# Regrouped start, adaLN rows, gates and boundary work in a two-layer hybrid transformer kernel, with the latent mean of each norm issued inside the last-but-one product

## The chip, the cores and the metric

The kernel runs on one core of one Trainium2 chip. The metric is the device time of one execution in microseconds. Before the change, three timed runs gave a median of 2119.14 us (2117.68 to 2120.08).

The core has five engines that run their own instruction streams: TensorE (PE in the profile, with PEld for its weight loads), VectorE (DVE), ScalarE (ACT), GpSimd (POOL) and SyncE (SP). An instruction waits in its engine's stream until the semaphores it names are reached, and everything behind it on that engine waits too. SP issues the transfers of almost all weights, POOL the transfers of the adaLN matrix.

## The reference

Two layers work on 256 latent tokens and 256 context tokens of width 1024. Cut to what matters:

```python
sc, scc = jax.nn.silu(c), jax.nn.silu(c_ctx)
for l in range(DEPTH):                                   # DEPTH = 2
    mod = (sc @ w_ada[l] + b_ada[l]).reshape(B, 1, 9, D) # and mod_c from scc, for the context
    h  = ffn_half_step(h, g_ffn1[l], mod[:,:,0], mod[:,:,1], mod[:,:,2], ...)   # and hc
    u  = modulate(rmsnorm(h, g_mix[l]), mod[:,:,3], mod[:,:,4])                 # and uc
    y, yc = token_mixer(u, uc, ...)      # u @ w_in -> attention, pooling, gated linear attention (GLA),
                                         # 3 x 1024 sigmoid gates; branches gated, summed, @ w_out
    h  = h + mod[:,:,5] * y                                                     # and hc, not in the last layer
    h  = ffn_half_step(h, g_ffn2[l], mod[:,:,6], mod[:,:,7], mod[:,:,8], ...)   # and hc, not in the last layer

def ffn_half_step(h, g, shift, scale, gate, w1, w3, w2):  # FF = 2816
    u = modulate(rmsnorm(h, g), shift, scale)
    return h + 0.5 * gate * ((silu(u @ w1) * (u @ w3)) @ w2)
```

Everything is float32. The output is the latent stream h.

## The kernel before, in words

**Layout.** The residual stream `h` lies transposed in SBUF: 8 tiles of 128 channels (k = 0..7), each with 512 columns, latent tokens first, context tokens behind. A product with a weight runs in three passes (`mm3`, lines 235 to 240): every float32 operand is split into a high part (made by ACT, line 190) and the rest (made by DVE, line 202), and TensorE adds high by high (L238), low of the data by high of the weight (L239), high of the data by low of the weight (L240). Data tiles are called uhi/ulo, hi/lo or oph/opl, weight tiles whi/wlo.

**Weights.** The class `Weights` is a planner: it records the order in which units of weights are asked for, and then loads ahead (SP issues the transfer into one of four raw buffers) and cuts ahead (ACT makes whi, DVE makes wlo) as long as the number of cut tiles stays under `room`. The rooms are `ROOM_FFN`, `ROOM_MIX`, and for the first FFN `ROOM_1` and `ROOM_2`. A framework with a list scheduler orders the instructions of each engine; it follows the order of the program text except where a dependency or a lower priority says otherwise. So a statement's place in the text decides where its instructions stand in each engine's queue.

**Stages.** In each layer ffn1, mixer, ffn2. An FFN runs 22 blocks of up-projections (`up`) in two halves, each followed by 8 down-products (`down`) that add to h (`grow`). The last two down-products, k = 6 and 7, run over the latent columns first and over the context columns second.

**Norms.** `grow` squares the new h tile on ACT and adds it to `acc` on DVE (L492). When h is complete, one product with a constant matrix gives the mean, `ms` (L508), ACT makes `rstd` from it (Ln, Exp), DVE makes `ut` (L517), ACT `uhi`, DVE `ulo` (L521). `norm_ahead` does the mean and rstd of the latent half while the context half of the last two products still runs; it is called after product k = 6 of the context span. The mixer's `out_last` does the same.

**adaLN.** `mod` needs 36 blocks (l, j) of 512 columns of `w_ada`. A generator (`ada_all`) does them in order, and calls of `adas(n)` all over the program move it n steps. The first four (l = 0, j < 4) are done on TensorE from rows loaded by SP: 8 float32 products 32x512 per block (L370), an ACT copy `adaev`, four transposes `ada2` (L384) and a DVE reduction. All the others are done on DVE (`adaacc`, L403, two per 128 rows) from rows loaded by POOL, with one 128x32 product at the end (L424), except those in the table `EDGE`: blocks (0,17) and (1,17) are done on TensorE like the first four, spread over the first products of ffn2 of each layer.

**Mixer.** Three generators are driven side by side: attention, GLA and a filler that spends TensorE's spare time on products of `w_in` and of the branches (psum tiles `fill`, `pool`). A table of credits `FILL` says how many filler steps go between two steps of attention or GLA; `GATES` says how many of the 8 middle gates (and 4 output gates) may be filled in before the pooling result is there. While the filler waits for attention (`len(self.oa) < 4`), it has nothing to give.

**The last FFN** covers the latent tokens only. Between its blocks 0 to 3 and the rest it transposes h to token-major (16 transposes, L715, copied by ACT into `ht`) and spreads the gate over the tokens (`gt`, L728).

## Time and profile before

| what | value |
|---|---|
| timed runs | 2119.14 us median (2117.68 to 2120.08) |
| profiled execution | 2120.19 us, span 2118.4 us |
| TensorE busy | 2071.1 us, 98% of the span |
| VectorE busy | 1449.1 us, 68% |
| ScalarE busy | 883.3 us, 42% |
| GpSimd busy | 138.4 us, 7% |
| granted TensorE clock, mean | 0.994 |

Times in the trace are counted from the start of the span. A group row reads: line, engine, operation, result from operands, shapes, count, busy time, mean duration in ns, idle time of the engine ahead of it and what ended it. Products are pipelined, so one that is shown 0.39 us long may start 0.23 us after the one before; a float32 (not split) product has two records.

### The profile page before, as it was taken

The page shows a single profiled execution, that of the slowest core. Times are in us where ns is not written, and L with a number is a line of the kernel's source. Part 1 is how long each engine was busy: PE and PEld are TensorE (multiplying, and loading weights), DVE is VectorE, ACT ScalarE, POOL GpSimd, SP SyncE. Part 2 cuts the span into 40 slices and gives each one's busy share as a digit, 9 for nine tenths or more (in the row PEclk, how much of TensorE's full clock was granted, in tenths as well). Part 3 has the DMA queues.
Part 4 walks back from the last instruction along what each step waited for, and adds up shares of the span by engine and source line. Part 5 has one row for each costly group of instructions (what it writes and reads, how often), then busy time and mean ns, then how long its engine had stood idle before and what let it go on. Part 6 is the DMA issues. An engine that isn't in the chain of part 4 may idle for free.

```text
span 2118.4 us, 30235 instructions
## 1 busy us (share of the span) xinstructions
PE 2071.1 (98%) x11308; PEld 1738.7 (82%) x11308; DVE 1449.1 (68%) x2876; ACT 883.3 (42%) x1805; POOL 138.4 (7%) x264
## 2 busy tenths in 40 slices
PE   7999999999999999999999999999999999998999
PEld 4888888977777888788888898888888887897997
DVE  4789588875877664766965886685554688665564
ACT  5423223464445553432322343322343566654452
POOL 0011011000100000101110100010000000000000
PEclk9999999999999999999999999999999999999999
DMA  9557456424423223445744645473451343565663
GB/s 319 150 157 206 125 170 169 118 59 122 137 75 83 67 70 95 130 139 139 216 132 131 173 125 154 110 224 114 121 151 36 102 119 85 140 169 145 182 205 121
DMA packets 416836, 290.48 MB, mean 137 GB/s; under 512 B 18608, under 2 KB 388912, under 8 KB 416688
## 3 DMA queue, kind: packets, MB, share of 16 engines
q1 hardware_dynamic: 395920, 221.22, 37.0%
q0 software_dynamic: 20480, 67.13, 11.1%
q8 instruction: 89, 1.46, 0.3%
q14 instruction: 59, 0.48, 0.1%
q10 hardware_dynamic: 288, 0.20, 0.0%
HBM read 287.44 MB, written 1.05 MB: 136 GB/s over the span
## 4 chain that ended last, share of the span: by engine, by line
PE 52%; issue 41%; DMA 3%; DVE 2%; POOL 1%; ACT 0%; SPq 0%; POOLq 0%; DVEq 0%; ACTq 0%
PE ps L238 14%; PE ps L240 14%; PE ps L239 14%; DMA raw<-in_w_ada_dram 2%; PE fill L238 2%; PE fill L240 2%; PE fill L239 2%; DMA ada<-in_w_ada_dram 1%; POOL raw L355 1%; PE sc L1145 1%; DVE adaacc L403 1%; PE ada L370 1%; PE pt L1163 0%; PE av L1181 0%; DVE wlo L202 0%
## 5 line engine op out<-in xcount | busy, mean ns | idle before, releaser
L202 DVE TENSOR_TENSOR wlo<-raw,whi 128x512 fp32r<-128x512 f32 (+4 forms) x912 | 532.5, 618 | 103.3 <-ACT whi L190 92.0
L238 PE MATMUL ps<-uhi,whi 128*128 128x512 f32 (+1 forms) x1584 | 555.4, 353 | 7.8 <-ACT uhi L190 7.8
L239 PE MATMUL ps<-ulo,whi 128*128 128x512 f32 (+1 forms) x1584 | 554.8, 351 | 0.2 <-DVE ulo L560 0.2
L240 PE MATMUL ps<-uhi,wlo 128*128 128x512 f32 (+1 forms) x1584 | 554.5, 351 | 0.0
L190 ACT ACTIVATE whi<-raw 128x512 fp32r<-128x512 f32 (+4 forms) x912 | 467.7, 567 | 173.6 <-DMA raw<-in_ffn_w_dram 53.7
L238 PEld LDWEIGHTS ps<-uhi,whi 128*128 128x128 f32 x1584 | 299.6, 190 | 54.1 <-ACT uhi L190 12.0
L240 PEld LDWEIGHTS ps<-uhi,wlo 128*128 128x128 f32 x1584 | 300.7, 190 | 46.1 <-issue 5.8
L239 PEld LDWEIGHTS ps<-ulo,whi 128*128 128x128 f32 x1584 | 300.9, 190 | 40.6 <-issue 1.9
L403 DVE SCALAR_TENSOR_TENSOR adaacc<-raw,csil,adaacc 128x512 f32<-128x512 f32 x420 | 303.9, 746 | 32.7 <-DMA raw<-in_w_ada_dram 32.1
L238 PE MATMUL ps<-hi,whi 128*128 128x512 f32 (+1 forms) x738 | 271.2, 368 | 1.5 <-ACT hi L190 1.5
L240 PE MATMUL ps<-hi,wlo 128*128 128x512 f32 (+1 forms) x738 | 269.9, 366 | 0.0
L239 PE MATMUL ps<-lo,whi 128*128 128x512 f32 (+1 forms) x738 | 269.6, 366 | 0.0
L190 ACT ACTIVATE silu<-ps 128x512 f32<-128x512 f32 (+1 forms) x88 | 47.8, 543 | 495.7 <-PE ps L240 495.7
L355 POOL DMA_DIRECT2D raw<-in_w_ada_dram x256 | 137.4, 537 | 1783.2 <-DVE adaacc L401 713.7
L659 DVE TENSOR_TENSOR silu<-silu,ps 128x512 f32<-128x512 f32 (+1 forms) x88 | 54.5, 619 | 245.7 <-PE ps L240 140.0
L238 PE MATMUL fill<-uhi,whi 128*128 128x512 f32 (+1 forms) x576 | 204.2, 355 | 3.9 <-ACT whi L190 3.9
L240 PE MATMUL fill<-uhi,wlo 128*128 128x512 f32 (+1 forms) x576 | 196.7, 342 | 0.2 <-DVE wlo L202 0.2
L239 PE MATMUL fill<-ulo,whi 128*128 128x512 f32 (+1 forms) x576 | 196.2, 341 | 0.0
L238 PEld LDWEIGHTS ps<-hi,whi 128*128 128x128 f32 x738 | 139.1, 189 | 24.0 <-ACT hi L190 1.7
L239 PEld LDWEIGHTS ps<-lo,whi 128*128 128x128 f32 x738 | 139.2, 189 | 22.6 <-DVE lo L202 0.2
L240 PEld LDWEIGHTS ps<-hi,wlo 128*128 128x128 f32 x738 | 139.2, 189 | 22.6
L238 PEld LDWEIGHTS fill<-uhi,whi 128*128 128x128 f32 x576 | 110.0, 191 | 26.2 <-issue 8.5
(279 smaller groups left out, 2304.8 us busy)
## 6 DMA issues: line engine op xcount, KB each, us to landing
raw<-in_ffn_w_dram SPq DMA_DIRECT2D x192, 512.0 KB, 4.7
raw<-in_w_ada_dram POOLq DMA_DIRECT2D x256, 256.0 KB, 3.4
raw<-in_w_in_dram SPq DMA_DIRECT2D x86, 512.0 KB, 4.5
raw<-in_ffn_w_dram SPq DMA_DIRECT2D x48, 384.0 KB, 4.4
raw<-in_ffn_w_dram SPq DMA_DIRECT2D x48, 320.0 KB, 3.8
raw<-in_w_branch_dram SPq DMA_DIRECT2D x48, 256.0 KB, 2.9
ada<-in_w_ada_dram SPq DMA_DIRECT2D x32, 256.0 KB, 5.4
raw<-in_w_out_dram SPq DMA_DIRECT2D x16, 512.0 KB, 5.0
```

The costliest lines, as they stand in the source:

```text
L190: i = self.nc.scalar.activation(**k)
L202: second = lambda: self.nc.vector.tensor_tensor(out=lo, in0=src, in1=f32hi, op=ALU.subtract)
L238: mm(out, wh, xh, start=start, stop=False)
L239: mm(out, wh, xl, start=False, stop=False)
L240: mm(out, wl, xh, start=False, stop=stop)
L355: self.nc.gpsimd.dma_start(out=t, in_=src)
L370: nc.tensor.matmul(ps[32 * g:32 * g + 32, :], self.csil[:, k, :], self.early[j][k] if early else unit.hi, start=(k < 4), stop=(k >= 4))
L403: nc.vector.scalar_tensor_tensor(out=acc[s], in0=unit.hi, scalar=c, in1=acc[s], op0=ALU.mult, op1=ALU.add)
L659: nc.vector.tensor_tensor(out=s[:, 0:n], in0=s[:, 0:n], in1=p3[:, 0:n], op=ALU.mult)
L1145: nc.tensor.matmul(sc[:, 0:nk], q[h][:, tt * P:(tt + 1) * P], keys[h][:, k0:T], start=True, stop=True)
```

## The change

The change does seven things.

1. **Start.** SiLU of the conditioning vector is made from Exp and DVE operations and not from the Silu table. The first adaLN block, the transposes that set up h, and the transposes of the normalised input come in another order, and the early adaLN blocks are tied into that order by dependencies. `ROOM_1` is 12, and the third unit of weights of the second half is asked for after k = 2 of the first products (`more`).
2. **Rows.** `EDGE` is empty: blocks (0,17) and (1,17) go through the DVE generator like the others.
3. **Gates.** `GATES` of mixer 0 is (4, ...) where it was 2. In mixer 1 a new `LATER` lets gates 0 to 7 and 16 to 23 run while the filler waits for attention.
4. **Boundary.** In the last FFN, the 16 transposes of h (`by_tokens`) come ahead of the norm, and the gate's products come after block 7 and not after block 3.
5. **Latent mean.** `norm_ahead` is called at f = 5 of 11 within the context span of down-product k = 6, and at k = 5 of 8 in the mixer's last output products, not after that product.
6. `ROOM_MIX` becomes a pair with the same two values.
7. Line numbers move: 190 becomes 191, 202 becomes 203, 238 to 240 become 239 to 241, 370 becomes 384, 384 becomes 400, 403 becomes 417, 508 becomes 522.

Three places in the engines' streams. First ScalarE at the start of the program, around the last two of the four early adaLN blocks (adaev; uhi is the first FFN's data, raw to whi the cutting of its weights). Before:

```order
L190 ACTIVATE whi<-raw 128x512 x2
L190 ACTIVATE uhi<-hr,mod_170,am_1_172 128x256 x6
L190 ACTIVATE whi<-raw 128x512 x4
L190 ACTIVATE adaev<-ada 128x512 x2
L190 ACTIVATE uhi<-hr,mod_170,am_1_172 128x256 x8
L190 ACTIVATE whi<-raw 128x512 x10
```

and after the change:

```order
L191 ACTIVATE whi<-raw 128x512 x2
L191 ACTIVATE uhi<-hr,mod_170,am_1_172 128x256 x6
L191 ACTIVATE whi<-raw 128x512 x2
L191 ACTIVATE adaev<-ada 128x512
L191 ACTIVATE whi<-raw 128x512 x6
L191 ACTIVATE adaev<-ada 128x512
L191 ACTIVATE uhi<-hr,mod_170,am_1_172 128x256 x8
L187 ACT_TABLE_LOAD
```

The first of the two adaev copies moved ahead of two cuts, the second moved behind four more. The six whi between them cut the three units of weights that follow.

Second TensorE in mixer 0, where the queries' norms (qsum) are turned (rq). Before:

```order
L238 MATMUL q<-hi,whi 128x512
L239 MATMUL q<-lo,whi 128x512
L240 MATMUL q<-hi,wlo 128x512
L1102 MATMUL qsum<-sqq,cst 32x512 x4
L1131 MATMUL rq<-cst_72,rq 128x128 x4
L238 MATMUL pool<-hi,whi 128x512
```

and after the change (the rows between these two pieces are further fill products, 24 in all between qsum and rq):

```order
L240 MATMUL q<-lo,whi 128x512
L241 MATMUL q<-hi,wlo 128x512
L1128 MATMUL qsum<-sqq,cst 32x512 x4
L239 MATMUL fill<-uhi,whi 128x512
L240 MATMUL fill<-ulo,whi 128x512
```

```order
L240 MATMUL fill<-ulo,whi 128x512
L241 MATMUL fill<-uhi,wlo 128x512
L1157 MATMUL rq<-cst_72,rq 128x128 x4
L239 MATMUL pool<-hi,whi 128x512
L240 MATMUL pool<-lo,whi 128x512
```

Two whole gates now stand between the sums and the turn.

Third TensorE at the boundary from mixer 1 to the last FFN, from the last output product (hilo) to the first up-products (uhi). Before:

```order
L240 MATMUL ps<-hilo,wlo 128x256
L508 MATMUL ms<-acc,cst_72 128x256
L370 MATMUL ada<-raw,csil 32x512 x3
L238 MATMUL ps<-uhi,whi 128x256 x4
L239 MATMUL ps<-ulo,whi 128x256
```

and after the change:

```order
L241 MATMUL ps<-hilo,wlo 128x256
L770 MATMUL ps<-cst_72,h 128x128 x16
L522 MATMUL ms<-acc,cst_72 128x256
L239 MATMUL ps<-uhi,whi 128x256 x3
L240 MATMUL ps<-ulo,whi 128x256
```

The adaLN products are gone from here (five more of them further on too), and the transposes of h stand where they were not before. At the same boundary of layer 0, the eight products of block (0,17) are gone in the same way.

The diff, cut to its core:

```diff
-ROOM_1, ROOM_2, LAST = 16, 36, 4
+ROOM_1, ROOM_2, LAST = 12, 36, 4
-GATES = (2, 12)
-EDGE = {(1, 17): (1, 2), (0, 17): (0, 2)}
+GATES = (4, 12)
+LATER = (0, 16)
+EDGE = {}
...
-        self.act(out=self.csil[:, :, 0:2], in_=self.vec[0][:, V_C:V_C + 16].rearrange("p (s k) -> p k s", s=2), func=AF.Silu)
+        c, e = self.vec[0][:, V_C:V_C + 16], self.tiny(16, "esil")
+        self.act(out=e, in_=c, func=AF.Exp, scale=-1.0)
+        nc.vector.tensor_scalar(out=e, in0=e, scalar1=1.0, scalar2=None, op0=ALU.add)
+        nc.vector.reciprocal(out=e, in_=e)
+        by_k = lambda t: t.rearrange("p (s k) -> p k s", s=2)
+        nc.vector.tensor_tensor(out=self.csil[:, :, 0:2], in0=by_k(c), in1=by_k(e), op=ALU.mult)
...
-        self.residual(range(4), [normed])
+        self.residual(range(6), (normed, last))
+        self.adas(4)
...
+        self.residual(range(6, KD))
+        self.xin = None
+        self.adas(1)
...
             self.evac = self.act(out=ev, in_=ps, func=AF.Copy)
-            if not early or j in (1, 3):
-                yield
+            yield
...
             self.w.room = ROOM_1
             first[0].extend(part(0, [2]))
-            first[1].extend(part(1, [0]))
+
+            def more():
+                self.adas(1)
+                self.w.room = 2 * ROOM_1
+                first[1].extend(part(1, [0, 1, 2]))
 
             def rest():
                 self.adas(1)
                 next(norm)
                 self.w.room = ROOM_2
-                first[1].extend(part(1, [1, 2]))
+                self.w.run_ahead()
 
         else:
             self.w.room = ROOM_FFN
+            ht = self.by_tokens() if final else None
...
-                    if c.start and k == 6:
-                        self.norm_ahead(l, i)
+                        if c.start and k == 6 and f == 5:
+                            self.norm_ahead(l, i)
...
-        up(0, 4)
+        up(0, 8)
+
         assert {(l, 8, 0), (l, 8, 1)} <= self.have
-
-        ht = []
-        ...
-        up(4, KF)
+        up(8, KF)
...
-                    if c.start and dc == dcs[0]:
-                        self.norm_ahead(l, 3)
+                        if c.start and dc == dcs[0] and k == 5:
+                            self.norm_ahead(l, 3)
...
+        later = [gate(j) for j in (*range(8), *range(16, 24))][0:LATER[l]]
         while len(self.oa) < 4:
-            yield 1
+            if later:
+                yield from later.pop(0)
+            else:
+                yield 1
...
-        for dc in range(4):
-            yield from gate(16 + dc)
+        for dc in range(4 if self.full else 8):
+            if 16 + dc not in self.gates:
+                yield from gate(16 + dc)
```

More of the change, by code (lines that the diff above doesn't have):

```diff
@@ L149, in __init__ @@
         self.have = set()
-        self.ahead = self.seconds = None
+        self.ahead = self.seconds = self.products = None
         self.after, self.owed, self.on_pe, self.edge = iter(()), 0, False, []
@@ L239, in mm3 @@
         mm(out, wh, xl, start=False, stop=False)
-        mm(out, wl, xh, start=False, stop=stop)
+        self.last_product = mm(out, wl, xh, start=False, stop=stop)
     def parts(self, src, n=T):
@@ L304, in setup @@
             self.act(out=f, in_=f, func=AF.Ln, scale=1.0 / D, bias=self.eps[:, 0:1])
-            self.act(out=f, in_=f, func=AF.Exp, scale=-0.5)
+            last = self.act(out=f, in_=f, func=AF.Exp, scale=-0.5)
             xr.append([self.slot(name="xr") for _ in range(2)])
@@ L367, in ada @@
                 for k in range(2 * u, 2 * u + 2):
+                    g = k % 4
                     unit = None if early else self.ada_unit(l, j, k)
-                    g = k % 4
-                    nc.tensor.matmul(ps[32 * g:32 * g + 32, :], self.csil[:, k, :], self.early[j][k] if early else unit.hi,
-                                     start=(k < 4), stop=(k >= 4))
+                    others = [self.last_product] if j in (1, 3) and not k else [self.products] if k else []
+                    self.products = nc.tensor.matmul(ps[32 * g:32 * g + 32, :], self.csil[:, k, :], self.early[j][k] if early else unit.hi,
+                                                     start=(k < 4), stop=(k >= 4))
+                    if early and self.tc:
+                        self.behind(self.products, others)
                     if unit:
@@ L621, in ffn @@
             self.adas(5)
-            self.residual(range(4, KD))
-            self.xin = None
-            self.adas(5)
             part = lambda half, ms: [self.both((w1, w3), 4 * half, m * P) for m in ms]
@@ L665, in up @@
                     if begin:
-                        steps = [lambda: None, lambda: self.adas(4), lambda: self.adas(1), lambda: self.adas(4), rest]
+                        steps = [lambda: None, lambda: self.adas(4), more, lambda: self.adas(4), rest]
                         o = self.dense_first(first, u, steps)
@@ L706, in ffn @@
             return
-        up(0, 4)
+        up(0, 8)
         assert {(l, 8, 0), (l, 8, 1)} <= self.have
-        ht = []
-        for j in range(2):
-            for c in range(2):
-                ps = self.ps()
-                for k in range(4):
-                    nc.tensor.transpose(ps[:, k * P:(k + 1) * P], self.h[:, 4 * c + k, j * P:(j + 1) * P], self.ident)
-                t = self.slot(name="ht")
-                self.act(out=t, in_=ps, func=AF.Copy)
-                ht.append(t)
         gt = []
@@ L753, in ffn, with by_tokens @@
         self.w.done(*us)
+    def by_tokens(self):
+        nc = self.nc
+        ht = []
+        for j in range(2):
+            for c in range(2):
+                ps = self.ps()
+                for k in range(4):
+                    nc.tensor.transpose(ps[:, k * P:(k + 1) * P], self.h[:, 4 * c + k, j * P:(j + 1) * P], self.ident)
+                t = self.slot(name="ht")
+                self.act(out=t, in_=ps, func=AF.Copy)
+                ht.append(t)
+        return ht
     def mixer(self, l):
@@ L761, in mixer @@
         self.l, self.full, self.n = l, full, n
[L762 removed]
+        self.w.room = ROOM_MIX[l]
         def load(t):
```

30 lines of the change are left out of this document (15 added, 15 removed).

## The prediction

> **What bounds the kernel now.** I read the page's busy times and its chain first, then TensorE's waits, then the granted clock in short windows.
>
> ```profile
> PE 2071.1 (98%) x11308; PEld 1738.7 (82%) x11308; DVE 1449.1 (68%) x2876; ACT 883.3 (42%) x1805; POOL 138.4 (7%) x264
> PE 52%; issue 41%; DMA 3%; DVE 2%; POOL 1%; ACT 0%; SPq 0%; POOLq 0%; DVEq 0%; ACTq 0%
> ```
>
> TensorE is busy for 98% of the span, and the chain lies on TensorE or on its issuing for 93%. So time comes off in three ways only: fewer instructions on TensorE, fewer waits of TensorE, or less time at a lowered clock. The waits (engine, line, what it waited for: total us, times, longest):
>
> ```profile
> PE ps L238 <- ACT uhi L190: 7.8, 6, 1.8
> PE ada L370 <- DMA raw<-in_w_ada_dram: 4.1, 2, 3.2
> PE fill L238 <- ACT whi L190: 3.9, 1, 3.9
> PE ms L508 <- DVE acc L492: 3.7, 1, 3.7
> PE rq L1131 <- ACT rq L190: 3.2, 1, 3.2
> PE ot L1383 <- DVE mx L1149: 1.7, 1, 1.7
> PE o L1367 <- DVE st L1352: 1.2, 1, 1.2
> ```
>
> These are small sums, but four of them are single waits over 3 us, and each of these costs more than itself. The windows show it (us, busy time of each engine, granted clock, DMA share, GB/s):
>
> ```profile
> 495.00:500.00 5.00, 5.00 (x19) 4.03 (x19) 3.15 (x7) 4.60 (x8) 0.00 (x0) 0.80 0.99 257
> 875.00:880.00 5.00, 3.30 (x8) 1.54 (x8) 4.86 (x15) 2.88 (x7) 0.73 (x2) 0.59 0.45 155
> 1700.00:1705.00 5.00, 3.62 (x16) 3.42 (x17) 5.00 (x13) 4.49 (x12) 0.00 (x0) 0.69 0.04 13
> 1910.00:1915.00 5.00, 4.03 (x14) 1.70 (x14) 3.39 (x8) 4.14 (x8) 1.59 (x3) 0.51 1.02 275
> 1915.00:1920.00 5.00, 4.04 (x13) 2.08 (x11) 3.83 (x9) 1.66 (x4) 0.54 (x1) 0.50 0.36 128
> 1235.00:1240.00 5.00, 5.00 (x44) 5.00 (x44) 5.00 (x11) 2.62 (x6) 0.54 (x1) 1.00 0.78 232
> ```
>
> The clock falls to about half behind the waits of 3.2, 3.2, 3.9 and 3.7 us and is 1.00 elsewhere; in the last window TensorE works undisturbed. What a low window costs is its busy time times the part of the clock that is missing: 1.0 us in the first (5.00 x 0.20).
>
> The Trainium skill (TensorE: Matmul & The Clock Gate, Part 1: The HAM clock gate) has the same behaviour with a window of about 3.4 us, both for falling to half and for coming back. Here 3.17 us was enough to fall. By the page a restart costs 1.7 us (half of 3.4).
>
> **The change part by part**, each against the span of 2118.4 us.
>
> *Rows (EDGE).* At the start of ffn2, TensorE works through the same stretch of 256-column up-products in layer 0, with block (0,17) between them, as ffn1 of layer 1 does without:
>
> ```profile
> 871.16 0.74 PE L238 MATMUL ps<-uhi,whi 128*128 128x256 f32 x4 [0.44 <-ACT uhi L190]
> 876.70 1.91 PE L370 MATMUL ada<-raw,csil 128*32 128x512 f32 x2 [3.17 <-DMA raw<-in_w_ada_dram]
> 905.69 0.48 PE L238 MATMUL ps<-uhi,whi 128*128 128x512 f32 x1
> 1248.89 0.74 PE L238 MATMUL ps<-uhi,whi 128*128 128x256 f32 x4 [1.43 <-ACT uhi L190]
> 1272.45 0.40 PE L238 MATMUL ps<-uhi,whi 128*128 128x512 f32 x1
> ```
>
> 905.69 - 871.16 = 34.53 us against 1272.45 - 1248.89 = 23.56 us. The difference, 10.97 us, is the products, their transposes, the 3.17 us wait for POOL's transfer and the slow clock behind it; all of it goes. Three of the eight products lie ahead of 871.16, where TensorE waits 0.44 us for uhi anyway; without them it only waits longer, so I count nothing for them. The work goes to DVE:
>
> ```profile
> L403 DVE SCALAR_TENSOR_TENSOR adaacc<-raw,csil,adaacc 128x512 f32<-128x512 f32 x420 | 303.9, 746 | 32.7 <-DMA raw<-in_w_ada_dram 32.1
> 1247.16 0.31 PE L424 MATMUL ada<-adapart,cst 128*128 128x32 f32 x2
> ```
>
> Two blocks are 32 operations of 0.746 us, 24 us on an engine that is idle for a third of the span. They stand at low priority, and the generator reaches them in ffn1 and the mixer of layer 1; that idle time is their cover, and without it they would cost up to 24 us. I take 0, and 0.4 us for the two small products (at most 0.31 each on TensorE). Term: **-11.0 + 0.4**.
>
> *Last FFN (block (1,17) and the 16 transposes).*
>
> ```profile
> 1905.78 0.28 PE L240 MATMUL ps<-hilo,wlo 128*128 128x256 f32 x1
> 1909.80 0.96 PE L508 MATMUL ms<-acc,cst 128*128 128x256 f32 x2 [3.74 <-DVE acc L492]
> 1913.59 1.22 PE L238 MATMUL ps<-uhi,whi 128*128 128x256 f32 x4 [0.97 <-ACT uhi L190]
> 1945.70 1.91 PE L715 MATMUL ps<-cst,h 128*128 128x128 f32 x16
> 1948.25 1.96 PE L728 MATMUL ps<-dg,ones 128*128 128x512 f32 x4 [0.64 <-DVE dg L727]
> ```
>
> From the first uhi product to the transposes are 32.1 us for 192 products of 256 columns. The same 192 products take 23.0 us where nothing disturbs them: the stretch of 23.56 us from 1248.89 above, less a mean of some 0.6 us that stands in it. The rest is the other five products of the block, their waits and the clock. After the change the transposes fill the wait ahead of ms (3.74 us holds their 1.91 us, and half of them need only tiles of h that are there), and ms and uhi come at about the same time as before: DVE has one cut less ahead of acc, ACT four copies more. With uhi at 1913.4, TensorE then stands still for some 3.5 us between ms and uhi, where before it had adaLN products. So I let the clock fall there: 4 us at half cost 2.1. Then 1913.4 + 23.0 + 2.1 = 1938.5, 7.2 us before 1945.70; the 1.91 us and the 0.64 us behind it go as well. Term: **-9.7**. Bounds: -6 if the copies hold uhi back by the 4 x 0.6 us that they take on ACT and more, -11.8 if the clock stays.
>
> *Gates in mixer 0.*
>
> ```profile
> 489.04 1.80 PE L1102 MATMUL qsum<-sqq,cst 128*32 128x512 f32 x8
> 494.02 1.12 PE L1131 MATMUL rq<-cst,rq 128*128 128x128 f32 x4 [3.18 <-ACT rq L190]
> ```
>
> TensorE waits here for Ln and Exp on ACT. After the change 24 fill products stand between, 5.5 us at full pace, longer than the wait of 3.18. Their weights are cut ahead by then. The wait goes, and with it the slow clock (1.0 us in the window quoted and 0.4 ahead of it). Term: **-4.6**.
>
> *Gates in mixer 1.* Fills now stand between the steps of attention, where TensorE waited 1.7 (ot) and 1.2 us (o). Both are shorter than one 12-product half of a gate of 256 columns (1.4 us) or about as long. Term: **-2.9**, bounds 0 and -3.4 (with the half microsecond of smaller waits there).
>
> *The latent mean.* It is meant to come earlier by 15 products in an FFN. At ffn2 of layer 0:
>
> ```profile
> 1242.14 0.42 DVE L492 TENSOR_TENSOR acc<-acc,sq 128x256 f32<-128x256 f32 x1
> 1242.74 0.63 PE L508 MATMUL ms<-acc,cst 128*128 128x256 f32 x2
> 1247.36 0.48 DVE L572 SCALAR_TENSOR_TENSOR h<-ps,am,h 128x256 f32<-128x256 f32 x1 [0.38 <-PE ps L240]
> 1247.83 0.46 DVE L517 SCALAR_TENSOR_TENSOR ut<-h,am,rstd 128x256 f32<-128x256 f32 x1
> ```
>
> 15 products are 1.8 us: ms would be due at 1240.94, but acc is there only at 1242.56, because DVE is full (5.00 of 5.00 in the window to 1240). TensorE then waits 1.6 us in the middle of a product, with the remaining context products queued behind. And nothing is won: ut stands on DVE behind the h of the last context product, which waits for TensorE itself, and DVE's order there is the same after the change. So the 1.4 us wait for uhi stays. At the other three boundaries acc comes earlier; I take 0.4 us for them together. Term: **+2.0**, bounds 0 and +4.
>
> *Start.* SP's transfers are in the same order, and they set the pace. What matters is when the last early adaLN block is done, since uhi for k = 4 to 7 needs it.
>
> ```profile
> 30.21 0.50 PE L238 MATMUL ps<-uhi,whi 128*128 128x512 f32 x1 [1.81 <-ACT uhi L190]
> 42.29 0.63 ACT L190 ACTIVATE whi<-raw 128x512 fp32r<-128x512 f32 x1 [0.20 <-DMA raw<-in_ffn_w_dram]
> 48.88 0.60 ACT L190 ACTIVATE adaev<-ada 128x512 f32<-128x512 f32 x1 [5.48 <-PE ada L370]
> 50.18 0.60 PE L384 MATMUL ada<-cst,adaev 128*128 128x128 f32 x4
> 45.08 0.92 SPq L229 DMA_DIRECT2D raw<-in_ffn_w_dram  x2
> raw<-in_ffn_w_dram SPq DMA_DIRECT2D x2, 256.0 KB, 3.6
> ```
>
> Before, adaev starts at 48.88 and its transposes at 50.18, with no wait of TensorE. After, it stands on ACT behind six whi. The last two of them wait for the two transfers issued from 45.08 to 46.0, which land 3.6 us later (the last row, the issues of just this window): the second at about 49.4. Then one cut of 0.63 and adaev of 0.60: the transposes can start at about 50.6, 0.4 us later than before. TensorE is earlier at this place, because its first products no longer stand behind as much (an estimate between 0 and 5 us; I take 4) and the other adaev is no longer behind a cut. It therefore waits here some 5 us, and then works 4 us at half clock, 2.1 us. Term: **+2.5**; bounds -3.7, if the wait isn't there and the early start is kept, and +4.
>
> *Sum:* -11.0 + 0.4 - 9.7 - 4.6 - 2.9 + 2.0 + 2.5 = **-23.3 us**. The profiled execution took 2120.19, its span 2118.4; the median of the runs is 2119.14, one microsecond below the former, so 2119.1 - 23.3 = **2096 us**.
>
> **The rivals.**
>
> 1. *A kinder start, or an earlier mean that pays.* If the start costs nothing or gains 3.7, or the waits for uhi (7.8 in all) shrink at three boundaries by up to 1.4 each: 2089 to 2093. For it: TensorE does start earlier. Against: ACT's order above, and DVE's order at the boundaries.
>
> 2. *Smaller gains.* In the last FFN uhi comes later (ACT has four more copies, -6 instead of -9.7), one or two of the new fills in mixer 1 stall, and the generator's extra work delays DVE where it is full. By 5 to 15 us less: 2101 to 2111.
>
> 3. *Slower: mixer 1's fills wait for their weights.* Each gate moved between attention's steps needs whi from ACT, which stands there behind the exponentials. One such wait is in the trace: 3.9 us for whi, and 1.1 us for the clock in the window from 1700 (3.62 x 0.31), 5 us together. 12 gates are filled in there (16 in `LATER`, less four that are left over). From five such waits on, nothing is left of 23; with eight it is 2096 + 40 = 2136. For it: the wait that exists, at exactly this kind of place. Against: it stands ahead of the part that changes, and the cuts run ahead of the fills.
>
> 4. *The change doesn't do what its title says.* The mean comes earlier, but ut can't start earlier. This I hold true, and it is in the sum as a loss. If it were without any stall as well, 2094, inside the forecast.
>
> By the Trainium skill's window (same page and section), a standstill just over 3 us is not always seen as idle. The last FFN's 3.5 us might then pass at full clock; the time would be 2094, which is inside the forecast too.
>
> **How the numbers follow.** Forecast (the sum, 2091 to 2101 with rival 4 in it): 0.62. Rival 1: 0.13. Rival 2: 0.18. Rival 3: 0.07, of which 0.03 lands within 0.2% of before (4 us, about what a measurement of this kernel can tell from no change) and 0.04 above. The time is that of the forecast, 2096. The range takes in rival 1 to 2088 and rival 2 to 2110: 0.88 by my chances, kept because the terms for the last FFN and the start each have bounds of 6 us. Faster 0.93, same 0.03, slower 0.04.
>
> **What would show it.** In the profile after: no wait of TensorE for in_w_ada rows; the stretch from the first uhi product of ffn2 in layer 0 to the first 512-column one at 23.6 us; no rq wait at 490; the stretch in the last FFN at 23 to 26 us; a new wait of about 1.6 us for ms behind acc at ffn2 of layer 0, with the uhi waits there unchanged; and a wait for adaev around 45 to 50 us with a lowered clock behind it. Wrong would be: uhi waits gone at the boundaries, waits of fills for whi in mixer 1, or a full clock from 45 to 55 us.

## The result, and the profile after

The changed kernel takes **2096.02 us** (median of 4 runs, 2095.41 to 2097.00) against 2118.74 us for the kernel before in the same comparison (2117.68 to 2120.08). The ratio is 0.9893, with a 95% interval of 0.9876 to 0.9910. The forecast was 2096 us. The profiled execution has a span of 2094.6 us, 23.8 us less than before. The sum is right to half a microsecond; several of its terms are not, and those are the subject here.

TensorE's waits in the profile after (engine, line, releaser: total us, times, longest):

```profile
PE ps L239 <- ACT uhi L191: 11.6, 6, 3.8
PE ada L400 <- ACT adaev L191: 3.9, 2, 3.1
PE fill L239 <- ACT whi L191: 3.9, 1, 3.9
PE ps L735 <- DVE dg L734: 1.9, 1, 1.9
PE ms L522 <- DVE acc L506: 1.1, 2, 0.6
PE ps L770 <- DVE h L586: 1.1, 1, 1.1
```

The waits for rq, ot, o and for the adaLN rows from POOL are gone. In their place stand a longer wait for uhi (3.8 us), one for adaev (3.1), one for the gate's diagonal tiles dg (1.9), and ms now waits for acc twice.

From TensorE's timeline of the same execution, the rows at which the stages begin:

```profile
50.62 0.66 PE L400 MATMUL ada<-cst,adaev 128*128 128x128 f32 x4 [3.12 <-ACT adaev L191]
404.40 0.74 PE L239 MATMUL ps<-uhi,whi 128*128 128x256 f32 x4 [1.60 <-ACT uhi L191]
868.05 0.74 PE L239 MATMUL ps<-uhi,whi 128*128 128x256 f32 x4 [1.43 <-ACT uhi L191]
891.61 0.40 PE L239 MATMUL ps<-uhi,whi 128*128 128x512 f32 x1
1235.35 0.75 PE L239 MATMUL ps<-uhi,whi 128*128 128x256 f32 x4 [1.43 <-ACT uhi L191]
1601.65 0.74 PE L239 MATMUL ps<-uhi,whi 128*128 128x256 f32 x4 [1.51 <-ACT uhi L191]
1888.29 0.28 PE L241 MATMUL ps<-hilo,wlo 128*128 128x256 f32 x1
1896.23 1.01 PE L239 MATMUL ps<-uhi,whi 128*128 128x256 f32 x3 [3.85 <-ACT uhi L191]
1947.38 1.98 PE L735 MATMUL ps<-dg,ones 128*128 128x512 f32 x4 [1.89 <-DVE dg L734]
```

The same rows of the trace before stand at 403.37, 871.16, 905.69, 1248.89, 1614.90 and 1905.78. So each stage can be compared:

| stage, from and to | before, us | after, us | change | forecast |
|---|---|---|---|---|
| start and ffn1 of layer 0, to the first product of mixer 0 | 403.37 | 404.40 | +1.03 | +2.5 |
| mixer 0, to the first product of ffn2 | 467.79 | 463.65 | -4.14 | -4.6 |
| first up-products of ffn2, layer 0 | 34.53 | 23.56 | -10.97 | -11.0 |
| rest of ffn2, to ffn1 of layer 1 | 343.20 | 343.74 | +0.54 | +1.6 (mean) |
| ffn1 of layer 1 | 366.01 | 366.30 | +0.29 | +0.4 (small products) |
| mixer 1, to its last output product | 290.88 | 286.64 | -4.24 | -2.9 |
| last FFN, to the end | 212.62 | 206.31 | -6.31 | -9.7 |
| mean at the three other boundaries, inside the stages above | | | | +0.4 |
| all | 2118.4 | 2094.6 | -23.8 | -23.3 |

The stretch without block (0,17) is exact to the hundredth, and the wait for adaev came at 50.62 where the forecast said "about 50.6". The last FFN gave 3.4 us less than forecast, mixer 1 and the start together 2.8 us more.

### The profile page after: what moved, and what is told of

Its sections match the earlier page's. It is cut to its first block, busy times and chain, and to the rows that moved or that the text cites. A ratio compares the mean times of both kernels' runs of the same rounds, so it can differ in the third digit from the quotient of the medians.

```text
span 2094.6 us, 30188 instructions
## 1 busy us (share of the span) xinstructions
PE 2055.1 (98%) x11272; PEld 1736.7 (83%) x11272; DVE 1475.8 (70%) x2923; ACT 881.8 (42%) x1802; POOL 138.9 (7%) x264
## 3 DMA queue, kind: packets, MB, share of 16 engines
HBM read 287.44 MB, written 1.05 MB: 138 GB/s over the span
## 4 chain that ended last, share of the span: by engine, by line
PE 68%; issue 13%; DVE 4%; DMA 2%; ACT 2%; POOL 1%; POOLq 0%; DVEq 0%; ACTq 0%
PE ps L239 15%; PE ps L241 15%; PE ps L240 15%; PE fill L239 5%; PE fill L241 4%; PE fill L240 4%; DMA raw<-in_w_ada_dram 2%; PE sc L1171 2%; POOL raw L368 1%; DVE wlo L203 1%; DVE adaacc L417 1%; PE av L1207 1%; PE gv L239 1%; PE pt L1189 1%; ACT whi L191 1%
## 5 line engine op out<-in xcount | busy, mean ns | idle before, releaser
L239 PE MATMUL ps<-uhi,whi 128*128 128x512 f32 (+1 forms) x1584 | 555.7, 353 | 11.6 <-ACT uhi L191 11.6
L417 DVE SCALAR_TENSOR_TENSOR adaacc<-raw,csil,adaacc 128x512 f32<-128x512 f32 x448 | 325.0, 747 | 32.4 <-DMA raw<-in_w_ada_dram 31.6
```

Of the source, the lines that this page charges most:

```text
L239: mm(out, wh, xh, start=start, stop=False)
L417: nc.vector.scalar_tensor_tensor(out=acc[s], in0=unit.hi, scalar=c, in1=acc[s], op0=ALU.mult, op1=ALU.add)
```

## The experiments

All are the changed kernel with one thing different, so the changed kernel's 2096.02 us (span 2094.6) is what they are compared with. Single times of one kernel lie within 1 to 4 us of each other; smaller steps are read from the stages of the traces.

**1. The mean put back.**

```diff
-                        if c.start and k == 6 and f == 5:
-                            self.norm_ahead(l, i)
+                    if c.start and k == 6:
+                        self.norm_ahead(l, i)
```

(and the same in the mixer's last output products.)

> The changed kernel with one thing undone: the latent mean is issued after the whole product k = 6 (and after the mixer's product), as before. Theory (the earlier mean buys nothing, since ut stands on DVE behind the last context h, and TensorE stalls for acc): the two waits of ms behind acc (0.60 us at 396 and 0.46 at 1227 in the changed kernel) go, the four waits for uhi of 1.4 to 1.6 us at the boundaries stay; about 1 us faster than the change, near 2095. Rival (the earlier mean feeds the next stage sooner): the waits for uhi grow by up to 1.5 us each at four boundaries, 2098 to 2102.

Measured: 2094.03 us (2093.39 to 2095.18), span 2092.6. That is 2.0 us faster than the change, with no overlap of the single times. The waits of the boundaries, in the trace of this kernel:

```profile
403.41 0.74 PE L239 MATMUL ps<-uhi,whi 128*128 128x256 f32 x4 [1.60 <-ACT uhi L191]
866.80 0.74 PE L239 MATMUL ps<-uhi,whi 128*128 128x256 f32 x4 [1.43 <-ACT uhi L191]
1233.43 0.74 PE L239 MATMUL ps<-uhi,whi 128*128 128x256 f32 x4 [1.43 <-ACT uhi L191]
1599.72 0.51 PE L239 MATMUL ps<-uhi,whi 128*128 128x256 f32 x2 [1.51 <-ACT uhi L191]
```

1.60, 1.43, 1.43, 1.51: the waits for uhi are the same to a hundredth of a microsecond wherever the mean stands. The part that gives the change its title buys nothing, and costs. It costs somewhat more than the two waits shown for ms (1.06 us): rows at the mean are also spaced wider than the shown wait explains. In ffn2 of layer 0 the product ahead of ms starts at 1226.75 and ms at 1227.48, 0.73 us with a shown wait of 0.46; with the mean put back ms follows the product ahead of it by 0.12. By the traces, the kernel with the mean put back is faster by 0.99 us to the first boundary (0.17 of it at the start), by 0.26 in mixer 0 and by 0.67 in ffn2 of layer 0.

**2. No gates kept for attention in mixer 1.**

```diff
-LATER = (0, 16)
+LATER = (0, 0)
```

> The changed kernel with no gates kept back for attention in mixer 1 (LATER = (0, 0)). Theory (the gates cover waits between attention's steps): the waits of ot and o (1.7 and 1.2 us before the change) come back and the stage from the first up-product of mixer 1 to its last output product gets 4.2 us longer, the step that the two traces show there; near 2100. Rival (mixer 1's gain comes from something else, its weights' order or the clock): no change in that stage, 2096.

Measured: 2102.43 us (2100.43 to 2102.66), span 2100.6. The mixer 1 stage is 4.8 us longer than in the change and the start 1.8 us, with a slow clock there (below); the other stages are together 0.5 us shorter. The two waits are back:

```profile
1780.12 0.43 PE L1393 MATMUL o<-st,qt 64*64 64x128 f32 x2 [1.16 <-DVE st L1378]
1792.10 0.41 PE L1409 MATMUL ot<-cst,sqo 128*128 128x128 f32 x2 [1.75 <-DVE mx L1175]
```

They are 2.91 us of the 4.8. The rest shows in a group of TensorE from 1765 to 1890 us, the products of attention with the values, first without the gates between, then in the changed kernel:

```profile
L1207 PE MATMUL av<-pT,v 128*64 128x256 f32 x64 | 9.7, 388 | 0.4 <-ACT p L191 0.4
```

```profile
L1207 PE MATMUL av<-pT,v 128*64 128x256 f32 x64 | 7.8, 385 | 0.4 <-ACT p L191 0.4
```

The same 64 products are busy for 9.7 us with other short products around them, and 7.8 us with gates between them. In the changed kernel they run in four groups of 16, of 1.95 us each where a row shows the whole group; here three of the four are split into 2 and 14, of 0.65 and 1.94 us, with products of o or of pt between the pieces. Why the pieces take longer is not shown by any run. The clock has a share too: behind the wait of 3.9 us for whi, which both traces have, the windows from 1685 to 1700 us lose 3.1 us here and 2.6 in the change (busy time times the missing part of the clock). So the waits are shown as the larger part of the 4.8 us; the rest is not split up cleanly.

**3. Two gates ahead of the pooling result in mixer 0.**

```diff
-GATES = (4, 12)
+GATES = (2, 12)
```

> The changed kernel with two gates and not four ahead of the pooling result in mixer 0. Theory (the two gates cover the wait for rq on ACT): a wait of about 3.2 us for rq comes back, with a lowered clock behind it; the stage between the first up-products of mixer 0 and of ffn2 in layer 0 gets 4.1 us longer; near 2100. Rival (the gain there comes from the boundary or the mean): 2096.

Measured: 2101.18 us (2100.06 to 2101.78), span 2098.9. The stage from the first products of mixer 0 to those of ffn2 is 468.20 us against 463.65, 4.55 longer. The wait is back to the hundredth:

```profile
495.59 0.66 PE L1157 MATMUL rq<-cst,rq 128*128 128x128 f32 x4 [3.18 <-ACT rq L191]
```

**4. The transposes of h put back.**

```diff
-            ht = self.by_tokens() if final else None
...
-        up(0, 8)
+        up(0, 4)
...
+        ht = self.by_tokens()
         gt = []
...
-        up(8, KF)
+        up(4, KF)
```

> The changed kernel with the 16 transposes of h in the last FFN back between blocks 3 and 4, together with the gate's products; block (1,17) stays on DVE. The prediction's reckoning (transposes and the wait for dg, 1.9 + 0.6 us, saved outright): 2.5 us slower, near 2098.5. Rival theory from the changed trace (the four copies of the transposes stand on ACT ahead of rstd, 1.57 us for three of them, and hold uhi back; the wait for dg moved and grew to 1.9 us): uhi comes about 1.5 us earlier, the transposes cost 1.9 on TensorE, the wait for dg shrinks by 1.3; no change or 1 us faster, 2095 to 2096.

Measured: 2097.05 us (2095.86 to 2097.83), span 2095.1: 1.0 us slower by the medians, with times that overlap, and 0.9 us longer from the last output product to the end. Both expectations miss by about as much. The timeline says why neither holds:

```profile
1892.46 1.22 PE L522 MATMUL ms<-acc,cst 128*128 128x256 f32 x2 [4.26 <-DVE acc L506]
1896.51 1.44 PE L239 MATMUL ps<-uhi,whi 128*128 128x256 f32 x5 [2.83 <-ACT uhi L191]
1922.31 1.91 PE L770 MATMUL ps<-cst,h 128*128 128x128 f32 x16
```

Without the transposes TensorE waits 4.26 us for acc and 2.83 for uhi; with them, 1.05 for h and 3.85 for uhi. The transposes fill the first wait as forecast, and ms comes 3.40 us after the last output product where it takes 4.55 without them. The second wait is longer by 1 us, but uhi does not come later for it: 7.94 us after the last output product with the transposes and their copies on ACT, 8.60 without. So the rival's theory, that the copies hold uhi back by 1.5 us, does not hold either. The clock falls to half afterwards in both (in the window from 1895 us, 0.50 here and 0.55 in the change).

**5. Block (0,17) put back on TensorE.**

```diff
-EDGE = {}
+EDGE = {(0, 17): (0, 2)}
```

> The changed kernel with adaLN block (0,17) back on TensorE at the start of ffn2 in layer 0 (block (1,17) stays on DVE). Theory: the stretch from the first uhi product there to the first 512-column product goes from 23.6 to 34.5 us, with the wait for POOL's transfer and the slow clock; 11 us slower, 2107. Rival (the 16 operations taken off DVE give something back elsewhere, at the waits for acc and uhi): 2102 to 2105.

Measured: 2108.59 us (2106.57 to 2109.58), span 2107.4, 12.8 more than the change. 1.7 of it are there at the first boundary already (406.09 against 404.40: the slow clock at the start, below). From the first products of ffn2 in layer 0 to those of ffn1 in layer 1 it takes 379.14 us against 367.30: 11.84 more, of which the wait of ms for acc there is 0.9 (1.37 against 0.46). What is left, 10.9, is the stretch (869.48 to 903.85 us, 34.37 against 23.56); its wait is back too:

```profile
874.97 1.91 PE L384 MATMUL ada<-raw,csil 128*32 128x512 f32 x2 [3.13 <-DMA raw<-in_w_ada_dram]
```

The other stages are together 0.7 us shorter, so taking the 16 operations away from DVE gave back 0.7 us at most, where the rival of 2102 to 2105 needs 4 us or more: it falls.

**6. The first FFN's weights in their old places.**

```diff
-ROOM_1, ROOM_2, LAST = 12, 36, 4
+ROOM_1, ROOM_2, LAST = 16, 36, 4
...
             first[0].extend(part(0, [2]))
+            first[1].extend(part(1, [0]))
...
-                self.w.room = 2 * ROOM_1
-                first[1].extend(part(1, [0, 1, 2]))
...
-                self.w.run_ahead()
+                first[1].extend(part(1, [1, 2]))
```

> The changed kernel with the old places and rooms of the first FFN's weights (so that ACT makes the last early adaev ahead of the six whi), but with the new order of transposes and adaLN blocks. Theory (adaev behind the cuts whose transfers land at 49.4 us costs the start): the wait for adaev (3.1 us at 50.6) goes and the transposes of that block come at about 47.5; 2 to 3 us faster, 2093 to 2094. Rival (the wait only moves, to the whi that now stand behind eight uhi, or the transfers set the pace anyway): 2096 or more, with new waits for whi or wlo between 50 and 65 us.

Measured: 2096.98 us (2095.12 to 2098.16), span 2095.2: no change. The first boundary comes at 404.42 against 404.40. The wait only moved to the adaev ahead of it, which now stands behind the cut of the unit that lands at 42 us:

```profile
43.79 0.66 PE L400 MATMUL ada<-cst,adaev 128*128 128x128 f32 x4 [2.62 <-ACT adaev L191]
50.51 0.60 PE L400 MATMUL ada<-cst,adaev 128*128 128x128 f32 x4
```

This does not yet tell "adaev behind a cut" from "the transfers set the pace whatever the order". Experiment 9 does.

**7. The first ut ahead of the last context h.** The norm's generator gets one more step, called inside the context product k = 7 (and in the mixer's last output product):

```diff
         for s, c in enumerate(streams):
             mean(c)
             yield u
-            some(s, c, range(KD))
+            if s == 0 and early:
+                some(s, c, range(early))
+                yield u
+            some(s, c, range(early if s == 0 else 0, KD))
             yield u
```

> The changed kernel with one more step: the first ut, uhi and ulo of the next norm's latent half (k = 0) are issued inside the context product k = 7 of an FFN (in the mixer: inside the last output product), so that they stand on DVE ahead of the last context h. Theory (what keeps uhi late is ut's place behind that h in DVE's queue): the four waits for uhi of 1.4 to 1.6 us at the boundaries go to below 0.4 each; 4 to 6 us faster, 2090 to 2092. Rival (uhi is late because of rstd on ACT, of mod, or of DVE's backlog): the waits stay or move to the second tile, 2095 to 2097.

Measured: 2111.09 us (2109.73 to 2112.91), 15 us slower. At the first boundary, from DVE's timeline and then from TensorE's:

```profile
400.19 0.47 DVE L531 SCALAR_TENSOR_TENSOR ut<-h,am,rstd 128x256 f32<-128x256 f32 x1
401.76 1.90 DVE L203 TENSOR_TENSOR wlo<-raw,whi 128x512 fp32r<-128x512 f32 x3
403.75 0.48 DVE L589 SCALAR_TENSOR_TENSOR h<-ps,am,h 128x256 f32<-128x256 f32 x1
406.49 0.48 DVE L531 SCALAR_TENSOR_TENSOR ut<-h,am,rstd 128x256 f32<-128x256 f32 x1
```

```profile
408.50 0.73 PE L239 MATMUL ps<-uhi,whi 128*128 128x256 f32 x4 [1.78 <-ACT uhi L191]
```

The first ut is early (400.19 where the changed kernel has 403.33), and the products with it run. But the edit also let the scheduler put the next stage's cuts further ahead: six wlo stand on DVE between the first ut and the second, which comes 6.3 us after the first, and TensorE waits 1.78 us for it. The 15 us come from several places: over the whole trace ms waits 5.6 us for acc where the change has 1.1, TensorE waits 14.3 us for uhi instead of 11.6, and the clock falls behind the new waits at three boundaries (0.66 in the windows from 410 and 1245 us, 0.50 and 0.82 in those from 1615 us), which loses 5.9 us. The run therefore does not settle what an earlier ut is worth alone; it shows that the wait moves to the second tile when the cuts come between.

**8. Three things in the last FFN.** The copies of the transposes on DVE; the Silu table kept behind all uhi; the diagonal tiles dg one block earlier:

```diff
-                self.act(out=t, in_=ps, func=AF.Copy)
+                nc.vector.tensor_copy(t, ps)
...
-                self.act(out=hi[:, c], in_=t, func=AF.Identity, bias=b)
+                self.users.append(self.act(out=hi[:, c], in_=t, func=AF.Identity, bias=b))
...
-        up(0, 8)
+        up(0, 7)
...
+        up(7, 8)
```

> The changed kernel with three things in the last FFN: the copies of the 16 transposes on DVE and not on ACT, the Silu table loaded behind all uhi and not ahead of them (at every norm), and the DVE operations of the gate (dg) one block earlier. Theory (ACT's copies, two cuts and the table load of 1.28 us make uhi late; the idle of 3.85 us behind the mean costs 2.9 us more in clock): the idle falls below 3 us, the clock stays near 1.00, the wait for dg (1.9 us) goes; 4 to 7 us faster, 2089 to 2092. Rival (DVE becomes what ut waits for, 4 copies of 0.7 us): idle over 3 us as before and only dg's 1.9 us gained, 2094.

Measured: 2093.31 us (2092.12 to 2095.28), span 2092.2 although its start had the slow clock; from the last output product to the end it is 2.8 us shorter than in the change. Only the small half came: the wait for dg is gone (1.9 us), the wait for uhi is 3.23 us, and the clock still falls. ACT's timeline at this place, first of the changed kernel, then of this one:

```profile
1891.09 1.57 ACT L191 ACTIVATE ht<-ps 128x512 f32<-128x512 f32 x3
1893.05 0.49 ACT L191 ACTIVATE rstd<-ms,eps 128x256 f32<-128x256 f32 x1
1893.93 0.43 ACT L191 ACTIVATE rstd<-rstd 128x256 f32<-128x256 f32 x1
1894.38 1.28 ACT L187 ACT_TABLE_LOAD   x1
1895.67 2.15 ACT L191 ACTIVATE uhi<-ut,mod 128x256 fp32r<-128x256 f32 x5
```

```profile
1894.06 0.42 ACT L191 ACTIVATE rstd<-rstd 128x256 f32<-128x256 f32 x1
1896.19 0.51 ACT L191 ACTIVATE uhi<-ut,mod 128x256 fp32r<-128x256 f32 x1 [0.67 <-DVE ut L531]
```

The 1.28 us of the table load are gone, but now uhi waits for ut, which stands on DVE behind the four copies (2.48 us). The rival was right about DVE; the gain is 0.9 us more than its 1.9.

**9. Another order at the start.** The changed kernel asks for all three units of the second half in `more`; here there is room for one of them ahead of the last early adaev, and the other two come behind it:

```diff
             def more():
                 self.adas(1)
-                self.w.room = 2 * ROOM_1
-                first[1].extend(part(1, [0, 1, 2]))
+                self.w.room = ROOM_1 + 4
+                first[1].extend(part(1, [0]))
 
             def rest():
                 self.adas(1)
+                self.w.room = 2 * ROOM_1
+                first[1].extend(part(1, [1, 2]))
                 next(norm)
```

> The changed kernel with one order at the start: ACT cuts only the unit of weights that is already there ahead of the last early adaev, and the other two units (whose transfers land at 48.5 and 49.4 us) behind it and ahead of the eight uhi. Theory (that adaev's place behind those cuts is what TensorE waits for): no wait for adaev between 40 and 51 us, its transposes at about 47.5; uhi then comes at about 51, when TensorE needs it; 3 us faster than the change, 2093. Rival (the transfers set the pace of the start, whatever the order): the wait moves to uhi or whi at 50 to 53 us and the time stays at 2096.

Measured: 2094.58 us (2093.25 to 2096.49), span 2091.5. No wait between 30 and 60 us, and the last early adaLN block is turned at

```profile
48.67 0.60 PE L400 MATMUL ada<-cst,adaev 128*128 128x128 f32 x4
```

1.95 us earlier than in the change. The first boundary comes at 402.23, 2.2 us earlier. So adaev's place behind the cuts is what TensorE waited for in the change. That the transfers set no pace does not follow. ACT starts the eight uhi at 51.31 us, only 0.64 earlier than in the change, and TensorE reached this place late in this trace: its clock from 25 to 35 us was 0.80 and 0.52. In experiment 11, with the same start and a full clock there, the wait that the rival named is seen:

```profile
52.76 0.50 PE L239 MATMUL ps<-uhi,whi 128*128 128x512 f32 x1 [1.19 <-ACT uhi L191]
```

By the times the gain is 1.4 us, and the single times overlap with those of the change.

**10. The transposes in two halves,** one ahead of the mean, one between the mean and uhi, with their copies on ACT, and the table and dg as in 8:

```diff
-            ht = self.by_tokens() if final else None
+            ht = self.by_tokens({}, 0) if final else None
             first = unit(0) + unit(1)
             u, rest = self.norm_go(l, i, n)
+            if final:
+                self.by_tokens(ht, 1)
```

> The changed kernel with four things in the last FFN: the transposes of h in two halves, one ahead of the mean and one between mean and uhi, so that neither stretch in which TensorE has nothing is 3 us long; copies on ACT; the Silu table loaded behind uhi; dg one block earlier. Theory (the idle stretch of 3.85 us and the slow clock behind it cost most of what the forecast's 9.7 us lacked): clock near 1.00 behind the boundary, uhi products at full pace; 5 to 6 us faster, 2090 to 2091. Rival (the clock falls by total busy time over a longer stretch and not by one idle stretch): clock at half again for 5 us or more; 2092 to 2093 (the 1.9 us of dg and 1 us of uhi only).

Measured: 2094.27 us (2093.12 to 2095.30), span 2091.4. The stage from the last output product to the end is 3.5 us shorter than in the change. TensorE's timeline, and then the windows behind it:

```profile
1892.85 0.70 PE L522 MATMUL ms<-acc,cst 128*128 128x256 f32 x2 [3.06 <-DVE acc L506]
1896.29 0.85 PE L239 MATMUL ps<-uhi,whi 128*128 128x256 f32 x5 [1.87 <-ACT uhi L191]
1897.75 0.29 PE L240 MATMUL ps<-ulo,whi 128*128 128x256 f32 x1
1898.27 0.41 PE L240 MATMUL ps<-ulo,whi 128*128 128x256 f32 x1
```

```profile
1895.00:1900.00 5.00, 3.71 (x23) 3.71 (x24) 5.00 (x14) 3.15 (x7) 0.00 (x0) 0.79 0.50 147
1900.00:1905.00 5.00, 5.00 (x39) 5.00 (x39) 1.63 (x5) 3.07 (x5) 0.00 (x0) 0.87 0.00 0
```

One of the two idle stretches is still 3.06 us long. The uhi products begin at full pace (0.29 us long) and slow down within 2 us (0.41): the clock fell anyway, after the idle stretches were over, and cost 3.71 x 0.21 + 5.00 x 0.13 = 1.4 us, half of what it costs in the change (2.85, below). The gain of 3.5 us in the stage is between the two expectations, nearer to the rival; the times stay above both, and the start of this trace had a slow clock. What makes the clock fall is not settled by this run.

**11. All together:** the mean put back (1), the start of 9 and the last FFN of 10.

> The changed kernel with the mean back behind its product (2.0 us by its own run), the start of x9_start and the last FFN of x10_tokens_split. If the three places are independent: the sum of their gains, 2 + 3 + 5 to 6 us, 2085 to 2086. If the start's gain or the boundary's gain isn't there: 2088 to 2091. If one gives back another (a wait that only moves): 2092 or more.

Measured: **2088.60 us** (2085.20 to 2089.50), ratio to the kernel before 0.9857 (0.9843 to 0.9872), span 2086.4. This beats both kernels: its slowest time lies 5.9 us below the fastest of the change. The gain over the change is 7.4 us by the medians; the sum of the three gains measured apart is 2.0 + 1.4 + 1.8 = 5.2 by the times. The 2085 to 2086 of three full gains did not come: each place gave something, but the start and the last FFN less than the expectation put in. Its waits:

```profile
PE ps L239 <- ACT uhi L191: 10.0, 7, 1.8
PE fill L239 <- ACT whi L191: 3.9, 1, 3.9
PE ms L522 <- DVE acc L506: 2.1, 1, 2.1
PE ada L400 <- ACT adaev L191: 0.8, 1, 0.8
```

Five waits for uhi of 1.0 to 1.6 us at the boundaries and the 3.9 us for whi in mixer 1 are what is left in the middle of the program; none of the runs touched the latter.

**The clock at the start, over all the runs.** The same wait for adaev at 50 us stands in nine of the traces, with different lengths. It ends at nearly the same time in all (50.35 to 50.82 us), but TensorE reaches the place at different times: its first products start between 28.66 and 29.62 us, and its clock between 25 and 35 us differs. The window behind the wait, in the changed kernel (wait 3.12 us) and in experiment 2 (wait 2.35 us):

```profile
50.00:55.00 5.00, 4.38 (x22) 3.69 (x23) 4.31 (x15) 3.62 (x9) 0.00 (x0) 1.00 1.13 296
```


```profile
50.00:55.00 5.00, 4.65 (x16) 3.82 (x17) 4.23 (x14) 3.47 (x8) 0.00 (x0) 0.66 1.14 295
```

The last three numbers are the granted clock (1.00 and 0.66), the DMA share and GB/s. A drop costs 4.65 x 0.34 = 1.6 us here, and it shows at the first boundary: in the kernels that leave the mean and the boundary as the change has them, 404.4 to 404.9 with a full clock, 405.8 to 406.2 with a slow one.

| wait for adaev, us | clock from 50 to 55 us | kernel |
|---|---|---|
| 1.74, 1.83, 2.04 | 1.00 | experiments 4, 7, 1 |
| 2.23, 2.26, 2.35 | 0.66 | experiments 8, 5, 2 |
| 3.12, 3.25 | 1.00 | the change, experiment 3 |
| 3.63 | 0.66 | experiment 10 |

So a longer wait does not mean a slower clock: 2.23 us was enough in one trace, and 3.25 us was not in another. These are single profiled executions; whether the same kernel falls into one or the other from run to run was not tried apart. Two other places say the same with waits of one length. Before the first products TensorE waits 0.80 us for adaev and 1.81 for uhi in all thirteen traces, and the clock from 30 to 35 us is then 1.00 in the kernel before and in experiments 10 and 11, 0.71 to 0.82 in the change and in experiments 1, 3 and 6, 0.66 in experiments 2, 4, 5, 7 and 8, and 0.52 in experiment 9. And the wait of 3.9 us for whi in mixer 1 is in all of them; the clock behind it costs 1.3 us in the kernel before and 1.2 to 3.1 us in the others. The Trainium skill (TensorE: Matmul & The Clock Gate, Part 1: The HAM clock gate) says that the window in which activity is counted runs freely and is not bound to the kernel's start. A cut by phase rather than by length agrees with the table, but no run here shows where a window begins. The same section of the Trainium skill lets the clock fall after at least one idle window of about 3.4 us; the drops after 2.23 to 2.35 us here do not agree with that, if the wait shown is all of the idle time.

## Why the prediction was right, and where its steps were wrong

The time is right to 0.02 us by luck, because errors cancel: the last FFN gave 3.4 us less than its term and mixer 0 0.5 less, while the start gave 1.5 us more, mixer 1 1.3 and the mean at ffn2 of layer 0 1.1. By the prediction's own steps:

- **Rows (-11.0 + 0.4): right.** 10.97 us forecast and 10.97 measured, and experiment 5 gives back 10.9 beside the wait of ms. The step that carried it was to price a stretch by the same stretch elsewhere in the same trace. That the 32 operations on DVE cost next to nothing is shown by experiment 5 for half of them: it takes 16 away, and 0.7 us at most is gained.
- **Gates in mixer 0 (-4.6): right.** -4.14 in the traces, of which the mean had taken back 0.26; experiment 3 brings back 4.55 us and the wait of 3.18. It also shows that this is the wait and the clock behind it together, as the term had it: the window from 495 us has 4.41 us busy at a clock of 0.66, which loses 1.5.
- **Gates in mixer 1 (-2.9): too small.** -4.24, past the bound of -3.4. The term counted the two waits, and these are what it says (2.91 in experiment 2). The bound had been made from waits alone; it left out that the same 64 av products are busy for 9.7 us without gates between them and 7.8 with them. And the stage hides some of the gain: the clock behind the wait for whi cost 2.6 us in the trace of the change and 1.3 in that of the kernel before. In experiments 8, 9 and 10, whose mixer 1 is that of the change, it costs 1.2 to 1.6 us and the stage takes 285.3 to 285.7 us, not 286.64. So with the clock as it was before, the term was too small by 2.3 to 2.7 us, an estimate from these stages, and not by 1.3.
- **The latent mean (+2.0): right in size and sign, wrong in its parts.** Putting it back gains 2.0 us. DVE's order was read rightly: the waits for uhi do not change by a hundredth. But the wait for acc at ffn2 of layer 0 is 0.46 us, not 1.6; another 0.6 us stands at the boundary ahead of mixer 0, where 0.4 us for three boundaries was set aside; and the rest lies in spacing around ms that no wait shows.
- **Start (+2.5): mis-sized.** The mechanism is the one described: adaev behind the cuts, its transposes at 50.62. But the first product was only 1.3 us early (28.90, before 30.21), not 4, and the clock from 25 to 35 us was 0.84 and 0.82, where it was full before; so the wait is 3.12 us and not 5. The 2.1 us for the clock behind the wait is the part that failed: in the profiled execution of the change it is 1.00 from 45 to 55 us, which the prediction had named as a sign of being wrong. (Its own figure is also a little high: 4 us at half are 2.0.) Of the +1.03 us at the first boundary 0.82 are the mean's, by experiment 1 (0.99 less 0.17), which leaves +0.2. In the traces where the clock fell behind the wait the boundary comes 1.4 to 1.8 us later still, nearer the term. Experiment 9 shows the mechanism from the other side: adaev 1.95 us earlier, the boundary 2.2 us earlier.
- **Last FFN (-9.7): the largest error.** It has -6.3. Three of its assumptions did not hold. The term let the clock be at half for 2.1 us of loss; the windows are

```profile
1895.00:1900.00 5.00, 3.77 (x17) 3.77 (x18) 4.86 (x13) 3.83 (x8) 0.00 (x0) 0.55 0.38 112
1900.00:1905.00 5.00, 5.00 (x36) 5.00 (x35) 1.61 (x5) 0.51 (x1) 0.00 (x0) 0.77 0.00 0
```

  that is 3.77 x 0.45 + 5.00 x 0.23 = 2.85 us. It let the 0.64 us wait for dg go; it grew to 1.89, and experiment 8, which makes dg one block earlier, takes it away. And uhi comes 7.94 us after the last output product, where 7.62 was forecast (1913.4 - 1905.78). Together 0.75 + 1.89 + 0.32 = 3.0 of the 3.4 us; the other 0.4 is not traced. The bound of -6 was met for another reason than the one it was given: it had the copies hold uhi back by 2.4 us and more, but uhi is 0.32 us late, and in experiment 4, without the copies ahead of it, it comes 0.66 us later still. What was missed is the clock and dg.

**The rivals.** Rival 1's start came half true (no gain of 3.7, but almost no loss either); its earlier mean that pays is ruled out by experiment 1. Rival 2 named the last FFN's -6, which came; its other parts did not. Rival 3 did not come: the trace after has one wait for whi of 3.9 us, the one that was there before. Rival 4 is shown by experiment 1: of what the title names, the rows and the gates bring the gain, and the mean takes 2 us of it back. That a standstill of over 3 us may pass at full clock, which the prediction gave to the last FFN, happened at the start; in the last FFN the clock fell in the trace of the change and in those of all experiments.

**What stays open.** For mixer 1, the two waits (2.91), the av products (1.9) and the clock (0.4) together are more than the 4.8 us of experiment 2, so they overlap or are counted in part twice; why the av products are busy for longer there was not tried by itself. What an earlier ut would be worth without the cuts that came along in experiment 7 is open too, and so is what decides the clock at the start. It accounts for part of the gap between experiment 11 and its parts: the trace of experiment 10 had the slow clock there, and its first boundary comes 1.4 us later than in the change, while that of 11 had a full one. By stages the parts are 1.8 (mean in 1, without the 0.17 at the start), 2.2 (first boundary in 9) and 3.5 (last stage of 10), 7.5 together, against 8.2 for the span of 11; the last stage gains 4.4 us there. The span of 9 gains 3.1, but 0.9 of that lies in mixer 1, which the edit does not touch and where the clock lost less.

## What to carry to other kernels

Price a piece of work that is to be moved by the same stretch of program with and without it in one trace: this gave the one term that was exact. Before a producer is moved ahead, read the queue of the engine between it and the product that waits: here ut stood on DVE behind an h that needs TensorE's last product, so that an earlier mean could bring nothing. Look for cuts that wait for a transfer and stand, in their engine's queue, ahead of a result that TensorE waits for: at the start, moving two units' cuts behind one such copy brought the product that needs it 1.95 us ahead, and was worth 1.4 us by the times. Before a gain of a microsecond or two is read from a stage, compare the granted clock of that stage in both traces: behind the same wait it cost between 1.2 and 3.1 us.

## What the runs showed of the hardware that was not expected

The clock does not follow the length of the idle time alone: full after waits of 3.12 and 3.25 us, 0.66 after 2.23, 2.26 and 2.35 at the same place of the program; between 0.52 and 1.00 from 30 to 35 us, behind waits of 0.80 and 1.81 us that are the same in every trace; and in experiment 10 it fell after the products had run for 1.6 us at full pace. The same 64 short products are busy for 9.7 us in groups that are split and 7.8 in whole ones. And a product that has to wait in the middle of others can cost more than the wait shown: 0.73 us between starts with a wait of 0.46, where the same product without a wait follows after 0.12.
